# A hybrid retention and RG-LRU layer: branch outputs summed by accumulating transfers, first merge job in seven products, rotary exchanges on ScalarE

## The chip, the core and the metric

The kernel runs on one core of a Trainium2 chip. The metric is the time of one execution on the device in microseconds (us); all times here are in us unless marked ns. The engines are TensorE (PE; its weight loads are shown apart as PEld), VectorE (DVE), ScalarE (ACT), GpSimd (POOL) and SyncE (SP). SP, ACT and POOL also issue transfers (DMAs), each from a queue of its own, and 16 DMA engines carry them out.

## The reference, cut to what matters

One layer over 1024 positions (T) and 1024 channels (D), all in float32:

```python
h = rms_norm(x, norm1_w)
q, k, v, g_ret, x_lru, y_lru, gate_ret, gate_lru = split(h @ w_in)
q = rotary(q); k = rotary(k) * 128 ** -0.5        # 4 heads of 128; halves [x1*cos-x2*sin, x1*sin+x2*cos]
o = chunkwise_retention(q, k, v)                  # chunks of 64, decayed state
y_a = (head_group_norm(o) * silu(g_ret)) @ w_ret_o
hl = rg_lru(conv4(x_lru))                         # gates, scan over positions
y_b = (hl * gelu(y_lru)) @ w_lru_o
mix = sigmoid(gate_ret + b0) * y_a + sigmoid(gate_lru + b1) * y_b
x = x + mix @ w_out
up = rms_norm(x, norm2_w) @ ffn_w_up              # D_FF = 3072
gate, val = split(up)
x = x + (gelu(conv3(gate)) * val) @ ffn_w_down
return rms_norm(x, norm_f_w)
```

## The kernel before, in words

**Products.** Each dense projection is cut into jobs; a job has a left side of 256 rows (or channels) and an operand on the right, both in 2 by 2 blocks (A11 to A22, B11 to B22). A product of two blocks is twelve matmuls of 128x128 by 128x512 into a PSUM bank: four steps of the contraction, three passes each, since every float32 value is split into a high part (a cast on ACT, L458) and the rest (a subtraction on DVE, L459). `mm_by` (matmuls in L669) makes the eight plain products of a job. `mm_fast` (L703) makes seven: from the blocks it uses sums S1 to S4 of the left side (formed on DVE, L544 to L553) and T1 to T4 of the right side. Intermediate sums are copied out of PSUM on ACT (L742) and added on DVE (L721, L727, in `total`). Two jobs can go as a pair (`mate`), product by product in turn. The lists PRODS, FIRST and ENDING are orders of the seven products.

**Stages, in order.** A few warming matmuls on constants (L1459); norm statistics and the values v (L1429); q and k projections, the rotary step and the retention heads, beside the projections of the LRU branch, with its gates and scan; the retention output jobs (`ojobs` 0 to 3) and the LRU output jobs (`ojobs` 4 to 7); the merge jobs (`wjobs`, one for each t from 0 to 3) with w_out and the residual; the MLP's up and down jobs; the last norm.

**Around the change.** `rotary_head` swaps the two halves of 64 partitions of each q and k tile by two transfers from POOL (L1165, L1166), multiplies by cosine and sine and adds (L1167 to L1169); k is then transposed on PE (L1177). `emit_ret_o` multiplies a tile of the retention output by its gate and stores it in t1_d. `emit_lru_o` reads it back (L1356), multiplies the LRU output by its gate (L1375), adds the two (L1376) and stores the sum into mix_d (L1378), the left side of the merge jobs, which load it at L510. The first merge job (t = 0) is plain; the other three have seven products. The parameters of the first norm are loaded by ACT's queue (L1453); the first use is L1414. At the end, each pair of down tiles is weighted and squared (`square`: DVE L1850, ACT L1852 with a sum along the row, DVE L1859), the power -1/2 is taken on POOL (L1863), and the tiles are scaled and stored (L1868 to L1871).

**What sets the order.** The program is built twice. From the first build, the class `Plan` takes every instruction with its dependencies: `latest` works back from PE's order to the time at which each step is due, `forward` then schedules all engines by these due times (`rank`) with modelled durations, and its order is imposed on the second build. Each engine executes its list in order. Work in the smaller PSUM banks (tiles named a: retention, gates, transposes) stands ahead of the dense products on PE when both are ready. SBUF tiles come from the pools u (128x512 work tiles) and w (blocks); PSUM tiles g and a.

Of the kernel before, what the change touches and what calls it, by code (L numbers as in the profile page):

```python
# [18 lines left out]
P = 128  # L19
# [106 lines left out]
class Step:  # L126

    def __init__(self, ins):
# [71 lines left out]
class Plan:  # L200
# [6 lines left out]
    LATE_DMA, LATE_PE, BACKLOG, KEEP = 1500.0, 400.0, 300.0, 2000.0  # L207
    NEAR, APART = 500.0, 10000.0
# [97 lines left out]
    def forward(self, rank):  # L306
# [7 lines left out]
        moved, table = 0.0, None  # L314
# [9 lines left out]
        while left:  # L324
# [28 lines left out]
            order[e].append(n)  # L353
            left -= 1
# [20 lines left out]
        return order, max(free.values())  # L375

    def order(self, rounds=2):
        pe = [n for n, s in self.steps.items() if s.eng == "PE"]
        for _ in range(rounds):
# [35 lines left out]
def tile_trunk_layer(ctx, tc, x, xt, positions, params, consts, normf, w_in, w_v, w_ro, w_lo,  # L415
# [26 lines left out]
    t1_d = pdr.tile([KT, P, T], F32, tag="t1", name="t1_d")  # L442
# [28 lines left out]
    class Job:  # L471
        def __init__(self, src, op, emit, post=None, fast=False, last=False, drop12=False,
                     pre=None, fetch=None, order=None, ready=None, by=None, rate=RATE, mate=False,
                     prods=PRODS, stage=None):
            self.pre, self.ready, self.by, self.rate = pre, ready, by, rate
            self.stage = stage
# [210 lines left out]
    def mm_fast(group, op):  # L687
# [5 lines left out]
        banks, kept = {}, {}  # L693

        def prod(jb, bank, nm):
# [3 lines left out]
            n = 0  # L699
            for j in range(4):  # L700
                c = slice(128 * j, 128 * j + 128)
                for a, b in PASSES:
                    PE.matmul(bank, w[a][:, c], need(op, (SETS[nm], j))[b], start=first and n == 0, stop=n == 11,  # L703
                              skip_group_check=True)
                    n += 1
# [9 lines left out]
        def total(jb, nm, bank, m, c):  # L715
            if back3:
                nm = {"S3": "S2", "S2": "S3"}.get(nm, nm)
            u = kept.pop((jb, nm))
# [8 lines left out]
            V.tensor_add(u, bank, u)  # L727
            jb.emit(m, c, u, u)

        for i, nm in enumerate(plan):  # L730
            for jb in group:
# [6 lines left out]
                bank = banks[key]  # L738
                prod(jb, bank, nm)
# [613 lines left out]
    def from_sg_t1(n):  # L1353
        def fetch(m, h):
            t = get()
            SY.dma_start(t, t1_d[2 * n + m, :, TH * h:TH * h + TH])  # L1356
            return from_sg(1, n)(m, h), t
        return fetch

    def emit_ret_o(n):  # L1360
        def emit(m, h, ps, unit):
# [3 lines left out]
            ST.dma_start(t1_d[ch, :, TH * h:TH * h + TH], t)  # L1365
# [5 lines left out]
    def emit_lru_o(n):  # L1371
        def emit(m, h, ps, unit):
            ch = 2 * n + m
            g, t = ojobs[4 + n].take(m, h)
            V.tensor_mul(g, ps, g)  # L1375
            V.tensor_add(t, t, g)  # L1376
            put(g)
            ST.dma_start(mix_d[2 * h:2 * h + 2, :, ch // 4, :, ch % 4, :].rearrange("t m p c -> p (t m) c"),  # L1378
                         t.rearrange("p (q c) -> p q c", q=4))
            put(t)  # L1380
# [5 lines left out]
    def values():  # L1386
# [66 lines left out]
        nc.scalar.dma_start(par[:, 0:8], params[:, 0:8])  # L1453
# [164 lines left out]
    for n in range(4):  # L1618
        ojobs.append(Job(pair_src(w_lo, n), u, emit_lru_o(n), fast=True, last=n == 3, mate=n == 0,
                         fetch=from_sg_t1(n)))  # L1620
# [239 lines left out]

    def final(t, m, c):
# [18 lines left out]
    def down_post(g, t):  # L1880
        def fn():
# [3 lines left out]
            if g == 1 and t == 3:  # L1885
# [5 lines left out]
                 prods=ENDING if (g, t) == (2, 3) else PRODS,  # L1891
                 pre=((0, 0), (0, 1), (1, 1)), fetch=from_x1(t),
# [70 lines left out]
```

## Time and profile before

| What | Value |
|---|---|
| Median of 3 runs (lowest to highest) | 1580.0 (1579.94 to 1580.3) |
| The profiled execution's own time | 1582.15 |
| Span of its trace | 1580.4 |
| Mean granted TensorE clock | 0.998 |
| DMA packets | 160976, 286.30 MB |
| Swaps of half tiles from POOL's queue (u<-u, 32 of the 40 in the rotary step), 128 KB each: issue to landing | 3.5 |
| Writes of mix_d, 16 of 256 KB | 5.2 |

The profile's page gives for each engine its busy time, share and instructions. In the chain of work that ended last a row is: start, length, engine, tile and line, count. In a timeline a row is: start, busy time, engine (a q behind it: its issue of transfers), line, operation, tile written <- tiles read, size, count, and in brackets the engine's idle time before it with what ended that. A group's row has the count, then busy time and mean ns of one, then idle time before. A row of transfers ends with the KB of each and the us from issue to landing.

### The profile page before, as it was taken

How to read it: one execution, taken by the hardware profiler on the slowest of the kernel's cores; microseconds unless marked ns; L12 is line 12 of the kernel's file. 1: busy time of each engine (PE TensorE's matmuls, PEld its weight loads, DVE VectorE, ACT ScalarE, POOL GpSimd, SP SyncE). 2: the span in 40 equal slices, each digit the busy share in tenths (PEclk: the TensorE clock that was granted, in tenths of full speed). 3: DMA queues.
4: the chain of work that ended last, by engine and by line, in shares of the span. 5: the costliest groups of instructions: out<-in, count | busy, mean ns of one | idle time of the engine just before them, and what ended most of it. 6: DMA issues, size and time to landing. Idle time of an engine off the chain costs nothing.

```text
span 1580.4 us, 21535 instructions
## 1 busy us (share of the span) xinstructions
PE 1566.9 (99%) x7001; PEld 1293.2 (82%) x7001; DVE 1368.3 (87%) x2462; ACT 912.6 (58%) x1554; POOL 67.9 (4%) x105
## 2 busy tenths in 40 slices
PE   9999999999999999999999999999999999999998
PEld 7888888888888888888888888888888888888886
DVE  8999988897889998999997899777777778987885
ACT  7548845544459697955365765444444446563653
POOL 0001010011000000000000001000000000000000
PEclk9999999999999999999999999999999999999999
DMA  9344354464454345684996246444444456787752
GB/s 324 116 121 144 117 171 132 156 205 148 126 180 158 96 146 185 222 274 165 304 388 225 91 131 210 134 146 139 135 140 140 142 190 213 267 274 270 261 182 80
DMA packets 160976, 286.30 MB, mean 181 GB/s; under 512 B 17880, under 2 KB 30304, under 8 KB 160864
## 3 DMA queue, kind: packets, MB, share of 16 engines
q1 hardware_dynamic: 153664, 264.74, 51.3%
q0 software_dynamic: 5760, 17.83, 3.9%
q10 hardware_dynamic: 1440, 2.36, 0.5%
q8 instruction: 55, 0.90, 0.2%
q14 instruction: 57, 0.47, 0.1%
HBM read 195.73 MB, written 83.89 MB: 177 GB/s over the span
## 4 chain that ended last, share of the span: by engine, by line
PE 94%; ACT 2%; DMA 2%; DVE 1%; issue 1%; POOL 0%; SPq 0%; POOLq 0%; ACTq 0%; DVEq 0%
PE g L703 82%; PE g L1429 5%; PE a L1105 3%; PE g L669 1%; PE a L1214 1%; DMA u<-u 1%; PE a L1216 1%; PE a L1225 1%; PE a L1208 0%; PE a L1275 0%; DMA u<-td_d 0%; PE a L1695 0%; DMA w<-mix_d 0%; DMA u<-xt 0%; ACT u L458 0%
## 5 line engine op out<-in xcount | busy, mean ns | idle before, releaser
L703 PE MATMUL g<-u,w 128*128 128x512 f32 x5964 | 1390.3, 391 | 1.5 <-ACT u L742 1.1
L703 PEld LDWEIGHTS g<-u,w 128*128 128x128 f32 x5964 | 1114.2, 188 | 232.1 <-ACT u L742 3.1
L458 ACT CAST w<-w 128x512 fp32r<-128x512 f32 x516 | 317.2, 621 | 364.0 <-PE g L703 250.4
L459 DVE TENSOR_TENSOR w<-w,w 128x512 fp32r<-128x512 f32 x516 | 350.8, 686 | 62.1 <-ACT w L458 56.4
L727 DVE TENSOR_TENSOR u<-g,u 128x512 f32<-128x512 f32 x213 | 145.8, 687 | 46.9 <-PE g L703 40.4
L458 ACT CAST u<-u 128x512 fp32r<-128x512 f32 x233 | 138.6, 621 | 69.4 <-PE g L703 7.4
L742 ACT COPY u<-g 128x512 f32<-128x512 f32 x215 | 125.0, 582 | 64.5 <-PE g L703 62.0
L459 DVE TENSOR_TENSOR u<-u,u 128x512 fp32r<-128x512 f32 x233 | 153.1, 685 | 4.5 <-ACT u L458 4.4
L1744 DVE SCALAR_TENSOR_TENSOR u<-u,par,u 128x511 f32<-128x511 f32 (+1 forms) x96 | 71.5, 747 | 3.0 <-ACT u L1741 2.6
L1429 PE MATMUL g<-w,u 128*128 128x512 f32 x264 | 61.9, 390 | 0.9 <-DVE u L1414 0.7
L1429 PEld LDWEIGHTS g<-w,u 128*128 128x128 f32 x264 | 49.3, 188 | 12.1 <-ACT w L458 1.2
L1749 POOL DMA_DIRECT2D ff_d<-u x48 | 36.2, 754 | 451.2 <-DVE u L1748 442.5
L544 DVE TENSOR_TENSOR w<-w,w 128x512 f32<-128x512 f32 x71 | 48.7, 685 | 2.9 <-DMA w<-ff_d 1.7
L1105 PE MATMUL a<-u,u 128*128 128x512 f32 x192 | 50.9, 391 | 0.3 <-ACT u L458 0.3
L547 DVE TENSOR_TENSOR w<-w,w 128x512 f32<-128x512 f32 x71 | 48.7, 687 | 0.8
L553 DVE TENSOR_TENSOR w<-w,w 128x512 f32<-128x512 f32 x71 | 48.6, 685 | 0.2
L550 DVE TENSOR_TENSOR w<-w,w 128x512 f32<-128x512 f32 x71 | 48.6, 685 | 0.2
L1741 ACT ACTIVATE u<-u,par 128x512 f32<-128x512 f32 x48 | 39.3, 818 | 15.1 <-DVE u L727 15.0
L721 DVE TENSOR_TENSOR u<-u,u 128x512 f32<-128x512 f32 x45 | 30.8, 687 | 16.8 <-ACT u L742 15.8
L1105 PEld LDWEIGHTS a<-u,u 128*128 128x128 f32 x192 | 35.5, 188 | 8.9 <-ACT u L458 1.0
L1748 DVE TENSOR_TENSOR u<-u,u 128x512 f32<-128x512 f32 x48 | 33.0, 689 | 5.9 <-ACT u L1747 5.8
L1087 DVE SCALAR_TENSOR_TENSOR u<-u,par,u 128x511 f32<-128x511 f32 (+2 forms) x48 | 35.8, 746 | 0.0
(202 smaller groups left out, 1125.1 us busy)
## 6 DMA issues: line engine op xcount, KB each, us to landing
w<-w_in SPq DMA_DIRECT2D x96, 256.0 KB, 2.8
w<-w_up SPq DMA_DIRECT2D x96, 256.0 KB, 2.7
u<-w_dn SPq DMA_DIRECT2D x84, 256.0 KB, 3.8
u<-x_d SPq DMA_DIRECT2D x60, 256.0 KB, 4.3
x_d<-u SPq DMA_DIRECT2D x48, 256.0 KB, 3.6
ff_d<-u POOLq DMA_DIRECT2D x48, 256.0 KB, 2.7
td_d<-u SPq DMA_DIRECT2D x48, 256.0 KB, 3.0
u<-td_d SPq DMA_DIRECT2D x48, 256.0 KB, 4.9
```

Source lines behind the costliest of these rows:

```text
L458: S.copy(hi, src)
L459: V.tensor_sub(lo, src, hi.bitcast(F32))
L544: V.tensor_add(s, r["A21"], r["A22"])
L547: V.tensor_sub(s, s, r["A11"])
L550: V.tensor_sub(s, r["A12"], s)
L553: V.tensor_sub(src, r["A21"], r["A11"])
L703: PE.matmul(bank, w[a][:, c], need(op, (SETS[nm], j))[b], start=first and n == 0, stop=n == 11, skip_group_check=True)
L727: V.tensor_add(u, bank, u)
L742: S.copy(u, bank)
L1105: PE.matmul(ps, wg[g][a][:, cs], xs[k][b], start=q == 0, stop=q == 5)
L1429: PE.matmul(bank, o[p][:, c], w[q], start=first and j == n == 0, stop=j == 3 and n == 2, skip_group_check=True)
L1744: V.scalar_tensor_tensor(c[:, s:], src[:, :TH - s], w, c[:, s:], ALU.mult, ALU.add)
```

## The change

- The first merge job gets seven products in place of eight, as a pair with the second, in the order FIRST; w_out's blocks are loaded in the order B11, T3, B21, T1, T2, T4, B22 (sums that an earlier stage kept in tw_d are read from there).
- `emit_ret_o` stores into mix_d, from SP; `emit_lru_o` adds its product to it by an accumulating transfer from POOL. The tensor t1_d, its 16 reads and the 16 adds on DVE are gone.
- The exchange of the rotary step is two copies on ACT.
- The parameters of the first norm are loaded by POOL's queue.
- The last product of the last down job is made in two halves of 256 columns in two fresh banks, and the last tile's norm (`final_half`) follows half by half, with its squares on DVE.
- The planner: float32r matmuls last (n + 32) / 2.4 ns instead of a fixed 226.6; a transfer's reader may stand closer to it; due times are mapped onto the start times that `forward` found.

```diff
-                t = 226.6
+                t = (n + 32) / 2.4
...
+    SURE_DMA = 700.0
...
                 lag = self.lag(s, self.steps[m])
                 if lag is not None:
+                    if s.dma:
+                        lag = max(self.HAND + self.SURE_DMA, min(lag, rank[m] - done))
                     at[m] = max(at[m], done + lag)
...
-            span = -min(start[n] for n in pe)
-            rank = {n: t + span - (1e7 if self.steps[n].small else 0.0) for n, t in start.items()}
-            order, _ = self.forward(rank)
+            due = np.maximum.accumulate([start[n] for n in pe])
+            if begin is None:
+                begin = due - due[0]
+            names = list(start)
+            found = np.interp([start[n] for n in names], due, begin)
+            found += np.minimum([start[n] for n in names] - due[0], 0.0)
+            rank = {n: t - (1e7 if self.steps[n].small else 0.0) for n, t in zip(names, found)}
+            order, begin = self.forward(rank)
...
+            for s in jb.halves if nm == plan[-1] and jb.halves else (slice(0, TH),):
+                if nm == plan[-1] and jb.halves:
+                    bank, first = psg.get(), True
+                    parts.append((s, bank))
...
+            if parts:
+                for s, part in parts:
+                    V.tensor_add(jb.sum[:, s], part[:, s], jb.sum[:, s])
+                    final_half(jb.sum, s)
+                return
...
-                G.dma_start(w[0:64, :], t[64:128, :])
-                G.dma_start(w[64:128, :], t[0:64, :])
+                S.copy(w[0:64, :], t[64:128, :])
+                S.copy(w[64:128, :], t[0:64, :])
...
+    def into_mix(ch, h, t, q, **how):
+        q.dma_start(mix_d[2 * h:2 * h + 2, :, ch // 4, :, ch % 4, :].rearrange("t m p c -> p (t m) c"),
+                    t.rearrange("p (q c) -> p q c", q=4), **how)
...
             V.tensor_mul(t, ps, t)
-            ST.dma_start(t1_d[ch, :, TH * h:TH * h + TH], t)
+            into_mix(ch, h, t, ST)
...
-            g, t = ojobs[4 + n].take(m, h)
+            g = ojobs[4 + n].take(m, h)
             V.tensor_mul(g, ps, g)
-            V.tensor_add(t, t, g)
+            into_mix(ch, h, g, G, accum_op=ALU.add)
...
-        nc.scalar.dma_start(par[:, 0:8], params[:, 0:8])
+        G.dma_start(par[:, 0:8], params[:, 0:8])
...
-        builders.append(operand(wop, w_out_set, False))
-        builders.append(kept_sums(wop, tw_d))
+        builders.append(operand(wop, kept_or(w_out_set, tw_d), False, ("B11", "T3", "B21", "T1", "T2", "T4", "B22")))
...
-                 emit_out(t, t > 0), out_post(t), fast=t > 0, last=t == 3, drop12=t == 0,
-                 pre=((0, 0), (0, 1), (1, 1)), fetch=from_x(t), by=None if t else "k",
-                 order=None if t else ("A11", "A21", "A12", "A22"),
+                 emit_out(t, True), out_post(t), fast=True, last=t == 3,
+                 pre=((0, 0), (0, 1), (1, 1)), fetch=from_x(t), mate=t == 0, prods=FIRST if t < 2 else PRODS,
...
+        V.scalar_tensor_tensor(j[:, s], u[:, s], 1.0 / D, u[:, s], ALU.mult, ALU.mult, accum_out=two)
+        V.tensor_add(one, one, two)
+        V.tensor_mul(o[:, s], u[:, s], nf[1][:, s])
+        if s.start == 0:
+            return
+        G.tensor_tensor(r, one, half[:, 0:1], ALU.pow)
...
+                 halves=(slice(0, TH // 2), slice(TH // 2, TH)) if (g, t) == (2, 3) else (),
```

**The exchange.** Before, POOL's queue, where the first rotary tiles (u) of one head are swapped; each row names the tile written and the tile read, and in brackets what it waits for (DMAHW and DMASW are transfers, the others engines):

```order
L1166 DMA u_421_2356<-u_413_2151 64x512 [waits DMAHW2_49,DMAHW1_49,DMAHW3_49,DMASW0_49,DMAHW4_49,DVE_49,Activation_49]
L1165 DMA u_421_2356<-u_413_2151 64x512 [waits DMASW1_49]
L1166 DMA u_428_2430<-u_418_2271 64x512 [waits DMAHW2_49,DMASW2_49,DMAHW5_49,DVE_49,PE_49]
L1165 DMA u_428_2430<-u_418_2271 64x512 [waits DMASW3_49]
L1166 DMA u_426_2404<-u_420_2316 64x512 [waits DMASW6_49,DMASW7_49,DMASW5_49,DMAHW1_49,DMASW4_49,Activation_49]
L1165 DMA u_426_2404<-u_420_2316 64x512
```

After, ACT's list at such a place. L1189 and L1190 are the two copies, L766 is the copy out of PSUM (L742 before), L468 the cast of a block (L458 before):

```order
L825 ACTIVATE rs<-rs 128x4 [waits DVE_49]
L468 CAST w_567_3213<-w_550_3027 128x512 [waits DMAHW3_49,PE_49,Activation_49]
L766 COPY u_508_3198<-g_97_2963 128x512 [waits PE_49]
L468 CAST w_563_3167<-w_558_3110 128x512 [waits DVE_49]
L1190 COPY u_541_3401<-u_495_3008 64x512 [waits DVE_49]
L1189 COPY u_541_3401<-u_495_3008 64x512
L766 COPY u_519_3277<-g_97_2963 128x512 [waits DMAHW7_49,PE_49]
L468 CAST w_571_3252<-w_513_2822 128x512 [waits DVE_49]
```

The two halves now stand in ACT's list between casts and PSUM copies, and wait for DVE alone.

**The merge.** Before, SP's list where the last sums are stored into mix_d and loaded (tw_d: kept sums of w_out; sg_d: gates):

```order
L1378 DMA mix_d<-u_1446_7853 128x4x128 [waits DMAHW7_49,DVE_49]
L1314 DMA u_1524_8007<-tw_d 128x512 [waits DMAHW0_49]
L1638 DMA u_1530_8014<-x 128x512 [waits DMAHW1_49]
L1349 DMA u_1406_7792<-sg_d 128x512 [waits DMAHW2_49]
L1378 DMA mix_d<-u_1380_7709 128x4x128 [waits DMAHW3_49,DVE_49]
L1314 DMA u_1535_8051<-tw_d 128x512 [waits DMAHW4_49,PE_49]
L1314 DMA u_1539_8057<-tw_d 128x512 [waits DMAHW5_49,PE_49]
L1314 DMA u_1543_8063<-tw_d 128x512 [waits DMAHW6_49]
L510 DMA w_1365_7930<-mix_d 128x512 [waits DMAHW7_49]
L510 DMA w_1377_7950<-mix_d 128x512 [waits DMAHW0_49]
L510 DMA w_1369_7936<-mix_d 128x512 [waits DMAHW1_49]
L510 DMA w_1381_7958<-mix_d 128x512 [waits DMAHW2_49]
```

After, SP's list where the last blocks of mix_d are loaded (L1656 loads tiles of x):

```order
L1656 DMA u_1542_8081<-x 128x512 [waits DMAHW3_49,DVE_49]
L1656 DMA u_1528_8043<-x 128x512 [waits DMAHW4_49,PE_49]
L1656 DMA u_1548_8156<-x 128x512 [waits DMAHW5_49,DVE_49]
L1656 DMA u_1549_8180<-x 128x512 [waits DMAHW6_49,DVE_49]
L1656 DMA u_1559_8275<-x 128x512 [waits DMAHW7_49]
L520 DMA w_1373_7906<-mix_d 128x512 [waits DMASW5_49,DMAHW0_49,DMASW4_49,DMASW1_49]
L520 DMA w_1375_7910<-mix_d 128x512 [waits DMAHW1_49]
L520 DMA w_1374_7908<-mix_d 128x512 [waits DMAHW2_49]
L520 DMA w_1380_7928<-mix_d 128x512 [waits DMAHW3_49]
L1656 DMA u_1550_8201<-x 128x512 [waits DMAHW4_49,DVE_49]
```

and POOL's last accumulating transfers ahead of that:

```order
L1378 DMA mix_d<-u_1379_7753 128x4x128 [waits DMAHW6_49,DMASW4_49,DVE_49]
L1378 DMA mix_d<-u_1419_7827 128x4x128 [waits DMAHW2_49,DMASW5_49,DVE_49]
L1378 DMA mix_d<-u_1359_7678 128x4x128 [waits DMAHW7_49,DMASW6_49,DVE_49]
L1378 DMA mix_d<-u_1444_7866 128x4x128 [waits DMAHW0_49,DMASW7_49,DVE_49]
L1378 DMA mix_d<-u_1380_7755 128x4x128 [waits DMAHW3_49,DMASW0_49,DVE_49]
```

The stores have left SP, and the first of the four loads waits for three transfers of POOL's queue (DMASW).

**The end.** Before, the last rows of DVE's list (u and nst are the tiles of the last norm; the g tiles are PSUM):

```order
L1834 TENSOR_TENSOR u60_2956_15280<-g4_465_15155,u60_2956_15280 128x512 [waits DMAHW4_49,DMAHW0_49,PE_49]
L1850 TENSOR_TENSOR u12_2977_15317<-u60_2956_15280,u26_2833_14660 128x512 [waits DVE_49]
L1859 TENSOR_TENSOR nst_80<-nst_80 128x1 [waits Activation_49]
L727 TENSOR_TENSOR u80_2933_15240<-g1_468_15244,u80_2933_15240 128x512 [waits PE_49]
L1850 TENSOR_TENSOR u36_2990_15341<-u80_2933_15240,u57_2834_14662 128x512 [waits DVE_49]
L1859 TENSOR_TENSOR nst_80<-nst_80 128x1 [waits Activation_49]
L1868 TENSOR_SCALAR u36_2990_15341<-u36_2990_15341,nst_80 128x512 [waits Pool_49]
```

After, the same place. L734 adds a half of the last product, L1883 squares and sums, L1885 weights, L1884 adds the sums:

```order
L1850 TENSOR_TENSOR u71_2906_15226<-g5_463_15101,u71_2906_15226 128x512 [waits DMAHW7_49,DMAHW3_49,PE_49]
L1866 TENSOR_TENSOR u21_2927_15263<-u71_2906_15226,u22_2783_14606 128x512 [waits DVE_49]
L1875 TENSOR_TENSOR nst_79<-nst_79 128x1 [waits Activation_49]
L734 TENSOR_TENSOR u31_2883_15186<-g2_470_15275,u31_2883_15186 128x256 [waits PE_49]
L1883 SCALAR_TENSOR_TENSOR u6_2941_15303,nst_79<-u31_2883_15186 128x256 [waits DVE_49]
L1885 TENSOR_TENSOR u25_2940_15302<-u31_2883_15186,u75_2784_14608 128x256
L1884 TENSOR_TENSOR nst_79<-nst_79 128x1 [waits DVE_49]
L734 TENSOR_TENSOR u31_2883_15186<-g4_471_15288,u31_2883_15186 128x256 [waits PE_49]
L1883 SCALAR_TENSOR_TENSOR u6_2941_15303,nst_79<-u31_2883_15186 128x256 [waits DVE_49]
L1885 TENSOR_TENSOR u25_2940_15302<-u31_2883_15186,u75_2784_14608 128x256
L1884 TENSOR_TENSOR nst_79<-nst_79 128x1 [waits DVE_49]
L1893 TENSOR_SCALAR u25_2940_15302<-u25_2940_15302,nst_79 128x512 [waits Pool_49]
```

The last tile's one add, one weighting and one sum have become two of each, with the squares among them.

More of the change, by code (lines that the diff above doesn't have):

```diff
@@ L313, in forward @@
         order = {e: [] for e in self.ENGINES}
-        moved, table = 0.0, None
+        moved, table, begin = 0.0, None, []
         for n, k in todo.items():
@@ L353, in forward @@
             order[e].append(n)
+            if e == "PE":
+                begin.append(t)
             left -= 1
@@ L441, in tile_trunk_layer @@
     sg_d = pdr.tile([2, KT, P, T], F32, tag="sg", name="sg_d")
-    t1_d = pdr.tile([KT, P, T], F32, tag="t1", name="t1_d")
     x1_d = pdr.tile([T, D], F32, tag="x1", name="x1_d")
@@ L473, in __init__ @@
                      pre=None, fetch=None, order=None, ready=None, by=None, rate=RATE, mate=False,
-                     prods=PRODS, stage=None):
+                     prods=PRODS, stage=None, halves=()):
             self.pre, self.ready, self.by, self.rate = pre, ready, by, rate
-            self.stage = stage
+            self.stage, self.halves = stage, halves
             self.mate, self.prods = mate, prods
@@ L698, in prod @@
             first = nm in ("A11", "S4" if over else "S1", "A12")
[L699 to L705, printed above, removed]
+            for s in jb.halves if nm == plan[-1] and jb.halves else (slice(0, TH),):
+                if nm == plan[-1] and jb.halves:
+                    bank, first = psg.get(), True
+                    parts.append((s, bank))
+                n = 0
+                for j in range(4):
+                    c = slice(128 * j, 128 * j + 128)
+                    for a, b in PASSES:
+                        PE.matmul(bank[:, s], w[a][:, c], need(op, (SETS[nm], j))[b][:, s],
+                                  start=first and n == 0, stop=n == 11, skip_group_check=True)
+                        n += 1
             W.put(*w, late=SOONER)
@@ L727, in total @@
             V.tensor_add(u, bank, u)
+            if jb.halves and (m, c) == (0, 1):
+                jb.sum = u
+                return
             jb.emit(m, c, u, u)
@@ L738, in mm_fast @@
                 bank = banks[key]
+                if jb.halves and nm == "S4":
+                    total(jb, "S2", bank, 0, 1)
                 prod(jb, bank, nm)
@@ L1859, in square, with final_half @@
             V.tensor_add(nst[:, 2, 2 + m:3 + m], nst[:, 0, 2 + m:3 + m], nst[:, 1, 2 + m:3 + m])
+    def final_half(u, s):
+        one, two, r = nst[:, 0, 2:3], nst[:, 4, 0:1], nst[:, 3, 2:3]
+        if s.start == 0:
+            fin["o"], fin["j"] = get(), get()
+        o, j = fin["o"], fin["j"]
+        V.scalar_tensor_tensor(j[:, s], u[:, s], 1.0 / D, u[:, s], ALU.mult, ALU.mult, accum_out=two)
+        V.tensor_add(one, one, two)
+        V.tensor_mul(o[:, s], u[:, s], nf[1][:, s])
+        if s.start == 0:
+            return
+        G.tensor_tensor(r, one, half[:, 0:1], ALU.pow)
+        put(u, j)
+        for c in range(2):
+            t = fin.pop((0, 0)) if c == 0 else o
+            if c:
+                V.tensor_scalar(t, t, r, None, ALU.mult)
+            else:
+                S.activation(t, t, AF.Copy, scale=r)
+            (SY if c else nc.scalar).dma_start(out[128 * 3:128 * 4, TH * c:TH * c + TH], t)
+            put(t)
     def final(t, m, c):
```

16 lines of the change are left out of this document (4 added, 12 removed).

## The prediction

> **What bounds the kernel now.** I read first the head of the page, then the chain of work that ended last, then the timelines at the places that the diff touches. All times are microseconds.
>
> ```profile
> span 1580.4 us, 21535 instructions
> PE 1566.9 (99%) x7001; PEld 1293.2 (82%) x7001; DVE 1368.3 (87%) x2462; ACT 912.6 (58%) x1554; POOL 67.9 (4%) x105
> PE 94%; ACT 2%; DMA 2%; DVE 1%; issue 1%; POOL 0%; SPq 0%; POOLq 0%; ACTq 0%; DVEq 0%
> ```
>
> TensorE is busy for 1566.9 of 1580.4, and 94% of the chain runs through it. So two things alone can shorten this kernel: fewer or cheaper matmuls, or the 13.5 in which TensorE stands. The next row, of the chain, prices a matmul; the others, of the timeline, show where TensorE stands at the start and the end.
>
> ```profile
> 904.47 433.54 PE g L703 x1912
> 1.25 4.55 PE L1459 MATMUL a<-heat 128*128 128x512 bf16 x12 [1.25 <-DVE heat L1623]
> 6.55 5.71 PE L1429 MATMUL g<-w,u 128*128 128x512 f32 x22 [0.74 <-DVE u L1414]
> 1553.82 18.98 PE L703 MATMUL g<-u,w 128*128 128x512 f32 x83
> ```
>
> 433.54 / 1912 = 0.2267 for one matmul of 512 columns. TensorE waits 1.25 before the warming matmuls and 0.74 behind them, and it ends at 1553.82 + 18.98 = 1572.80, so 7.60 of the span lies behind it. Three waits in between, quoted below, make 0.95, 1.07 and 0.87. Together that is 12.48 of 13.5: what is left for the new planner to win anywhere else is about 1.0.
>
> **Part 1, the first merge job as seven products.** One product of twelve matmuls goes. TensorE is the bound on both sides of it: 12 x 0.2267 = **-2.72**. The four loads of w_out that go with it had no wait of their own.
>
> **Part 2, the norm weights from GpSimd's queue.**
>
> ```profile
> 0.74 0.41 ACTq L1405 DMA_DIRECT2D u<-xt  x1
> 1.18 0.45 ACTq L1453 DMA_DIRECT2D par<-params  x1
> 1.66 1.28 ACT L1456 ACT_TABLE_LOAD   x1 [1.66 <-PEq L1948]
> 5.92 0.48 DVE L1414 TENSOR_SCALAR u<-u,par 128x512 fp32r<-128x512 f32 x1 [4.72 <-DMA par<-params]
> par<-params ACTq DMA_DIRECT2D x1, 4.0 KB, 4.6
> u<-u POOLq DMA_DIRECT2D x40, 128.0 KB, 3.5
> ```
>
> The first real matmul waits for L1414, and L1414 for the parameters, issued at 1.18 as ScalarE's second transfer and landed 4.6 later. No small transfer from GpSimd stands in this trace. By its nearest row, the exchanges (3.5), and an issue at about 0.75, as ScalarE's first (0.74), the parameters land at 4.25. Then the warming matmuls, which end at 1.25 + 4.55 = 5.80, decide: the 0.74 is gone, **-0.74**. Ends: the longest landing of an exchange is 7.0 (quoted below), which from 0.75 ends at 7.75 instead of 5.8, +1.9; nothing earlier than 5.80 helps.
>
> **Part 3, the rotary exchanges on ScalarE.**
>
> ```profile
> 339.43 0.63 PE L1177 MATMUL a<-cst,u 128*128 128x128 f32 x4 [0.95 <-DVE u L1169]
> 402.54 0.66 PE L1177 MATMUL a<-cst,u 128*128 128x128 f32 x4 [1.07 <-DVE u L1169]
> L458 ACT CAST u<-u 128x512 fp32r<-128x512 f32 x233 | 138.6, 621 | 69.4 <-PE g L703 7.4
> 230.00:440.00 210.00, 207.99 (x995) 173.96 (x994) 181.59 (x414) 98.21 (x186) 13.36 (x26) 1.00 0.50 154
> DMA to landing us min/median/max: 2.5/4.2/7.0
> ```
>
> (The fourth row is the table of windows: length, then busy time of PE, PEld, DVE, ACT and POOL, clock, DMA share, GB/s; the last is the landing of the exchanges of L1165.) Twice TensorE stands before a transpose of a rotated tile, because an exchange lands late. A pair of copies takes about 2 x 0.62 = 1.24, by ScalarE's SBUF-to-SBUF cast of as many columns (half the partitions, which I count for nothing), where the transfer took 4.2 in the middle. Both waits should close: 0.95 + 1.07 = **-2.02**. The price is 32 x 0.62 = 19.8 of ScalarE's time, in a window where it is busy for 98.2 of 210; with them it is 118 of 210, so TensorE's work covers it. The cover is gone where a copy waits in ScalarE's order with a copy out of PSUM behind it: ends 0 and, if every one of the eight tiles costs TensorE a copy's 0.62, +5.0. DVE keeps its three instructions for each tile.
>
> **Part 4, the chain into the merge.** Now DVE no longer adds the two branches: the LRU product goes into mix_d by an accumulating transfer, and the merge loads wait for it.
>
> ```profile
> 793.76 0.61 PE L669 MATMUL g<-u,w 128*128 128x512 f32 x2
> 794.62 0.58 ACT L742 COPY u<-g 128x512 f32<-128x512 f32 x1
> 795.25 5.76 PE L703 MATMUL g<-u,w 128*128 128x512 f32 x24 [0.87 <-ACT u L742]
> 799.06 0.68 DVE L1375 TENSOR_TENSOR u<-g,u 128x512 f32<-128x512 f32 x1
> 800.26 0.69 DVE L1376 TENSOR_TENSOR u<-u,u 128x512 f32<-128x512 f32 x1
> 800.97 0.37 SPq L1378 DMA_DIRECT2D mix_d<-u  x1
> mix_d<-u SPq DMA_DIRECT2D x16, 256.0 KB, 5.2
> w<-mix_d SPq DMA_DIRECT2D x16, 256.0 KB, 5.3
> ff_d<-u POOLq DMA_DIRECT2D x48, 256.0 KB, 2.7
> ```
>
> The old order's wait of 0.87 in front of the merge goes with that order. What is late next is the second half of mix for rows 0 to 255. From the end of the matmuls of LRU channel block 7 (first rows) the chain is: PE to its reader 0.25 (794.37 to 794.62), multiply 0.68, issue 0.02 (800.95 to 800.97), the accumulating transfer, the load 5.3, a sum of two blocks on DVE 0.69, its cast 0.62, and three hand-overs at an estimated 0.1 each: 7.86 plus the transfer. In the new PE order 55 matmuls stand between those and the first product that reads it: 55 x 0.2267 = 12.47 of cover. No accumulating transfer is in the trace. With the old write of the same tile, 5.2, the chain is 13.06 and TensorE waits 0.6; net of 0.87 **-0.27**. Ends: a landing like ff_d's of the same shape on the same queue, 2.7, leaves no wait (-0.87); twice the old write, 10.4, gives 7.86 + 10.4 - 12.47 = 5.8, net +4.9. I take 5.2, since the same stage's load decides it. Queued behind an accumulate on GpSimd are only more accumulates; behind the four waiting loads on SP, loads of x for the sums of the merge, which are late by as much.
>
> **Part 5, the last product in halves.**
>
> ```profile
> 1571.66 0.16 DVE L1859 TENSOR_TENSOR nst<-nst 128x1 f32<-128x1 f32 x1
> 1572.84 0.69 DVE L727 TENSOR_TENSOR u<-g,u 128x512 f32<-128x512 f32 x1 [1.02 <-PE g L703]
> 1575.04 0.16 DVE L1859 TENSOR_TENSOR nst<-nst 128x1 f32<-128x1 f32 x1 [0.79 <-ACT a L1852]
> 1575.28 0.54 POOL L1863 TENSOR_TENSOR nst<-nst,half 128x1 f32<-128x1 f32 x1 [2.78 <-DVE nst L1859]
> 1575.86 0.72 ACT L1870 ACTIVATE u<-u,nst 128x512 f32<-128x512 f32 x1 [0.85 <-POOL nst L1863]
> 1576.61 0.34 ACTq L1871 DMA_DIRECT2D out<-u  x1
> L1229 DVE SCALAR_TENSOR_TENSOR state<-state,a 128x256 f32<-128x256 f32 x24 | 9.8, 410 | 0.5 <-PE a L1225 0.4
> L926 DVE DVE_READ_ACCUMULATOR a<-u 128x1 f32 x8 | 1.1, 141 | 0.0
> L703 PEld LDWEIGHTS g<-u,w 128*128 128x128 f32 x5964 | 1114.2, 188 | 232.1 <-ACT u L742 3.1
> ```
>
> With the first half ready half a product early, DVE starts at 1571.82, when the last norm step of the tile before it ends, and works through two halves: 2 x (add 0.41 + square 0.41 + read-out 0.14 + weight 0.41 + sum 0.16) = 3.06, and nine gaps of 0.03: 1575.15, against 1575.20 now. The sum, the power and the scaling behind it stay: **-0.05**. That holds if 24 matmuls of 256 columns cost half each, 24 x 0.113 = 2.72. If the weight load sets the pace, 24 x 0.188 = 4.51; the second half then ends at 1574.59 instead of 1572.80, and DVE's second half at 1576.29: +1.1. A gain of more than 0.3 is excluded by DVE's own row of work.
>
> **Part 6, the planner.** The new table moves retention work a few dozen matmuls earlier and lets a reader stand closer to its transfer (0.7 instead of up to 1.5). I count it as nothing: at most 1.0 is to be won, and five readers that each come 0.8 early would lose 4. Two more activation table loads (1.28 each, by the row quoted in part 2) lie in ScalarE's idle time.
>
> **Sum:** -2.72 - 0.74 - 2.02 - 0.27 - 0.05 = -5.80. The span becomes 1574.6. The profiled execution took 1582.15 with its 1580.4 of span, the median of the runs is 1580.0; a change in the span carries over: **1574.2**.
>
> **Rivals.**
>
> **(a) The accumulating transfers fill the transfer engines: slower.**
>
> ```profile
> q1 hardware_dynamic: 153664, 264.74, 51.3%
> q0 software_dynamic: 5760, 17.83, 3.9%
> 690.00:780.00 90.00, 90.00 (x399) 74.52 (x398) 89.05 (x148) 43.87 (x76) 0.00 (x0) 1.00 0.74 244
> 780.00:840.00 60.00, 59.13 (x260) 48.39 (x259) 52.66 (x88) 35.10 (x66) 0.72 (x1) 1.00 1.05 380
> ```
>
> 256 KB take all 16 engines 0.513 x 1580.4 x 0.262 / 264.74 = 0.80 on SP's queue and 0.91 on GpSimd's. From 780 to 840 the share is 1.05: here there is no room. The change takes out 16 reads, 16 writes and 4 loads, 36 x 0.80 = 28.8, and puts in 16 accumulates of an unknown length e. At e up to 1.8, twice a plain one, it breaks even. Slower by over 0.2% (3.2, about what a measurement of this kernel can tell from no change) needs the whole gain of 5.8 eaten and 3.2 more, 9.0 of transfer time: e = (28.8 + 9.0) / 16 = 2.4, three times a plain one. At four times, 3.2, the excess is 16 x 3.2 - 28.8 = 22 and the time 1596, less what the emptier stage before 780 takes up. For it: pieces of 512 bytes, each read and written. Against it: the loads fall by 20, and the share before 780 is 0.74. Chance 0.11.
>
> **(b) ScalarE's order takes back what the exchanges gave.** The copies stand in one queue with the casts and the PSUM copies; the two waits return as waits for ScalarE, and the planner's closer readers add one or two. Then the gain of part 3 is nil and 1 to 4 are lost: 1577 to 1580, said as 1578. For it: ScalarE is in order. Against it: its idle 112 of 210. Chance 0.20.
>
> **(c) Descriptors written late.** DVE is busy 89.05 of 90 before the merge. If GpSimd's transfers are held while DVE works, an accumulate lands like the slowest exchange, 7.0: the chain is 14.86, the wait 2.4 instead of 0.6, the time 1576.0. For it, 7.0 with DVE at 86%; against it, ff_d's 2.7 with as busy a DVE. Chance 0.08. The Trainium skill states such a rule on its page "SBUF — State Buffer", section "Who interferes with whom": GpSimd must write the descriptors of its transfers, and DVE in a two-port mode locks it out, which two-tensor operations do not do. By that rule part 4 would cost 1.8 more than by the row of 5.2; ff_d's row speaks against it, and no run here isolates it.
>
> **(d) The halves are bound by weight loads**: +1.1, 1575.3, inside the forecast's own spread.
>
> **How the numbers follow.** The forecast with its spread, 1572.5 to 1576.5, has 0.53; better than that, by a shorter merge chain and the planner's 1.0, 0.08; (c) 0.08; (b) 0.20; (a) 0.11. Faster by over 0.2% means below 1576.8: 0.53 + 0.08 + 0.08 = 0.69. Within it: 0.20. Slower: 0.11. The range, 1571.5 to 1581.5, leaves out (a)'s slow end, the merge chain's 10.4 together with another loss, and a sliver below.
>
> **What would show it.** 24 fewer matmuls of 512 columns and 24 of 256 in their place; the first matmul behind the warming ones at about 5.8 instead of 6.55; no idle time before the transposes of rotated tiles; the wait before the first merge product that reads the second half of mix (0.6), and the landing of the accumulates beside 5.2; the transfer share around the merge; the last product's matmuls at 0.113 each and the last output's issue near 1571. I am wrong if the accumulates take more than 2.4 of engine time, if ScalarE becomes the releaser in front of TensorE, or if TensorE's idle time grows at places that the diff does not name.

## The result, and the profile after

The changed kernel takes 1592.89 (median of 4 runs, 1591.83 to 1594.84), the kernel before 1580.15 (1579.94 to 1581.64): a ratio of 1.0078, 95% interval 1.0066 to 1.0091. It is slower by 12.7, where 5.8 less had been forecast, and outside the range of 1571.5 to 1581.5. The profiled execution took 1591.83 with a span of 1590.1, 9.7 more than before.

The head of the page and the queue of GpSimd's transfers:

```profile
span 1590.1 us, 21467 instructions
PE 1569.2 (99%) x7001; PEld 1295.0 (81%) x7001; DVE 1368.9 (86%) x2464; ACT 934.1 (59%) x1588; POOL 72.9 (5%) x90
q0 software_dynamic: 12704, 17.83, 5.0%
```

The slices of the page show where to look: the granted TensorE clock is 9 in every slice but one, around 800. TensorE's timeline there (start, busy time, operation, count, and in brackets the idle time ahead with its releaser):

```profile
763.68 24.53 PE L717 MATMUL g<-u,w 128*128 128x512 f32 x107
796.38 21.91 PE L717 MATMUL g<-u,w 128*128 128x512 f32 x84 [8.17 <-ACT u L766]
822.03 8.24 PE L717 MATMUL g<-u,w 128*128 128x512 f32 x28 [3.73 <-ACT w L468]
```

Two waits, 8.17 and 3.73, stand where the kernel before has one of 0.87. And the matmuls behind them are slow: 84 in 21.91 are 2.87 more than 84 x 0.2267, and 28 in 8.24 are 1.89 more. The windows of the trace (length, then busy time of PE, PEld, DVE, ACT and POOL, clock, DMA share, GB/s) put it on the granted clock, which is 0.50 in the 5 us behind the first wait and 0.57 in the mean of the 4 behind the second:

```profile
796.40:801.40 5.00, 5.00 (x12) 3.93 (x13) 5.00 (x10) 3.57 (x7) 0.98 (x1) 0.50 1.05 387
801.70:817.90 16.20, 16.20 (x72) 13.41 (x71) 11.43 (x20) 8.90 (x16) 5.11 (x4) 0.99 1.14 255
822.00:826.00 4.00, 3.97 (x10) 3.04 (x11) 3.99 (x7) 3.56 (x7) 0.00 (x0) 0.57 1.02 379
```

Who makes TensorE wait? ScalarE's timeline and its waits in this stage (what it waited for: us in total, times, longest):

```profile
777.10 0.57 ACT L766 COPY u<-g 128x512 f32<-128x512 f32 x1
789.32 0.62 ACT L468 CAST w<-w 128x512 fp32r<-128x512 f32 x1 [11.64 <-DMA w<-mix_d]
...
795.75 0.57 ACT L766 COPY u<-g 128x512 f32<-128x512 f32 x1
```

ScalarE stands for 11.64 at the cast of a block of mix. The copy out of PSUM that TensorE's next product needs (795.75) is behind it in the list, with nine more casts between. That block is late because its load is issued at 782.34 and lands 6.9 later; the load stands in SP's list behind loads that wait for accumulates in flight (first row, SP's waits; run 10 shows that the data would have held it as long), and the accumulates land late (second and third row: the transfers of the whole trace and the landings of the lines of L1378, stores from SP included):

```profile
SPq L1355 <- DMA mix_d<-u: 7.4, 1, 7.4
mix_d<-u POOLq DMA_DIRECT2D x16, 256.0 KB, 8.4
DMA to landing us min/median/max: 2.3/6.0/13.1
```

The second wait is the chain that the prediction had worked out, here from the chain of work that ended last:

```profile
807.14 8.42 DMA mix_d<-u
...
815.70 4.91 DMA w<-mix_d
820.61 0.02 issue
820.63 0.70 DVE w L554
821.34 0.02 issue
821.36 0.63 ACT w L468
821.98 0.04 issue
822.03 8.01 PE g L717 x27
```

Accumulate 8.42, load 4.91, sum 0.70, cast 0.63, and TensorE goes on. The other parts of the change, at the start, in the retention stage and at the end:

```profile
1.25 5.30 PE L1477 MATMUL a<-heat 128*128 128x512 bf16 x12 [1.25 <-DVE heat L1641]
1.28 0.71 POOL L1471 DMA_DIRECT2D par<-params  x1 [0.83 <-POOLq L1987]
5.89 0.49 DVE L1432 TENSOR_SCALAR u<-u,par 128x512 fp32r<-128x512 f32 x1 [4.69 <-DMA par<-params]
230.00:440.00 210.00, 210.00 (x1007) 176.14 (x1007) 184.21 (x420) 118.46 (x218) 0.00 (x0) 1.00 0.45 144
1580.51 0.69 DVE L1850 TENSOR_TENSOR u<-g,u 128x512 f32<-128x512 f32 x1 [0.59 <-PE g L717]
1581.74 1.60 PE L717 MATMUL g<-u,w 128*128 128x256 f32 x12
1582.12 0.42 DVE L734 TENSOR_TENSOR u<-g,u 128x256 f32<-128x256 f32 x1
```

The parameters land at 5.89, as before. The warming matmuls end at 1.25 + 5.30 = 6.55, where the prediction had 5.80. In the retention stage TensorE is busy for 210.00 of 210 (207.99 before). From the add of the last whole product (1580.51; 1570.12 in the trace before) to the end of the span it is 1590.1 - 1580.51 = 9.59, and 1580.4 - 1570.12 = 10.28 before. The 24 half matmuls lie in this stretch: they start at about 1580.45 and end at 1581.74 + 1.60 = 1583.34, 0.12 each.

| Part | Forecast | From the two traces |
|---|---|---|
| 12 matmuls fewer | -2.72 | -2.72 |
| Start | -0.74 | -0.03 (6.52 for 6.55) |
| Exchange: the two waits | -2.02 | -2.02 |
| Merge: waits (8.17 + 3.73 for 0.87) | -0.27 | +11.03 |
| Merge: half clock behind them (2.87 + 1.89) | not foreseen | +4.76 |
| End, the 24 halves included | -0.05 | -0.69 |
| Sum | -5.80 | +10.33; the span shows +9.7, and the 0.6 between them was not placed |

### The profile page after: what moved, and what is told of

Read it like the earlier page. It is cut to its first block, busy times and chain, and to the rows that moved or that the text cites. A ratio compares the mean times of both kernels' runs of the same rounds, so it can differ in the third digit from the quotient of the medians.

```text
span 1590.1 us, 21467 instructions
## 1 busy us (share of the span) xinstructions
PE 1569.2 (99%) x7001; PEld 1295.0 (81%) x7001; DVE 1368.9 (86%) x2464; ACT 934.1 (59%) x1588; POOL 72.9 (5%) x90
## 3 DMA queue, kind: packets, MB, share of 16 engines
q0 software_dynamic: 12704, 17.83, 5.0%
## 4 chain that ended last, share of the span: by engine, by line
PE 47%; issue 2%; DMA 1%; DVE 1%; POOL 1%; ACT 0%; POOLq 0%; SPq 0%; ACTq 0%; DVEq 0%
PE g L717 47%; POOL mix_d L1378 1%; DMA mix_d<-u 1%; DMA u<-sg_d 1%; PE a L1713 0%; DVE w L469 0%; DMA w<-mix_d 0%; DVE u L1396 0%; DVE u L469 0%; DVE u L1385 0%; ACT u L468 0%; DVE u L746 0%; ACT u L1722 0%; DVE w L554 0%; DVE u L920 0%
## 5 line engine op out<-in xcount | busy, mean ns | idle before, releaser
L717 PE MATMUL g<-u,w 128*128 128x512 f32 x6060 | 1413.2, 392 | 12.5 <-ACT u L766 8.4
L717 PEld LDWEIGHTS g<-u,w 128*128 128x128 f32 x6060 | 1133.9, 188 | 246.6 <-ACT u L766 9.9
L468 ACT CAST w<-w 128x512 fp32r<-128x512 f32 x519 | 318.3, 621 | 368.1 <-PE g L717 250.1
L766 ACT COPY u<-g 128x512 f32<-128x512 f32 x218 | 126.9, 582 | 66.7 <-PE g L717 64.9
L468 ACT CAST u<-u 128x512 fp32r<-128x512 f32 x229 | 134.7, 620 | 52.5 <-PE g L717 5.3
L1378 POOL DMA_DIRECT2D mix_d<-u x16 | 20.5, 1400 | 657.6 <-DVE u L1396 638.0
```

Of the source, the lines that this page charges most:

```text
L468: S.copy(hi, src)
L717: PE.matmul(bank[:, s], w[a][:, c], need(op, (SETS[nm], j))[b][:, s], start=first and n == 0, stop=n == 11, skip_group_check=True)
L766: S.copy(u, bank)
```

## The experiments

The theories at the outset. **A:** an accumulating transfer is slow, and what waits for it makes both waits. **B:** the pair of seven-product jobs asks for mix too early, however it is written. **C:** the new planner puts readers too close to their transfers. Each run's kernel is the changed one, but for the edit shown. The runs of the kernel before beside them had medians of 1580.80 (the first four), 1581.24 (the next four) and 1581.33 (the last four); ratios are to those runs, with 95% intervals.

**1. Plain writes in place of the accumulates.** The retention branch is missing from mix. Every engine's list is the same, row by row and buffer by buffer, as in the changed kernel; the 16 transfers alone differ.

```diff
-            into_mix(ch, h, g, G, accum_op=ALU.add)
+            into_mix(ch, h, g, G)
```

> The changed kernel with the 16 accumulating transfers as plain writes from the same queue, at the same place of every engine's list; it leaves the retention branch out of mix. Theory A (an accumulating transfer is slow: about 2.0 us of all 16 transfer engines instead of 0.9, landing 8.8 in the merge instead of about 5): the two waits of TensorE in the merge (8.2 and 3.7) shrink to under 2 together, the granted clock there stays at 1.00, and the time falls to 1574 to 1578. Theory B (the pair of seven-product jobs asks for mix too early, and ScalarE stands before the cast of a block of mix with TensorE's copies behind it, however the transfer writes): both waits stay over 8 together and the time stays at 1588 or above.

Measured: 1578.88, ratio 0.9986 (0.9977 to 0.9995). GpSimd's queue, the landing of its writes, and TensorE in the merge:

```profile
q0 software_dynamic: 5536, 17.83, 3.6%
mix_d<-u POOLq DMA_DIRECT2D x16, 256.0 KB, 5.3
789.30 4.38 PE L717 MATMUL g<-u,w 128*128 128x512 f32 x18 [1.44 <-ACT u L766]
794.21 15.26 PE L717 MATMUL g<-u,w 128*128 128x512 f32 x66 [0.52 <-ACT u L766]
810.43 19.86 PE L717 MATMUL g<-u,w 128*128 128x512 f32 x85 [0.97 <-ACT w L468]
```

The waits are 1.44, 0.52 and 0.97, the 85 matmuls behind the last one run at 0.234. One word in one line is worth 14.0: theory A holds, since neither order nor buffers differ. The time is still not 1574; 2.9 of waits remain that the kernel before does not have in this form.

**2. The add on DVE again** (t1_d, its reads, the stores from SP).

```diff
-            into_mix(ch, h, g, G, accum_op=ALU.add)
+            V.tensor_add(t, t, g)
+            into_mix(ch, h, t, ST)
```

> The changed kernel with the two branches added on DVE as before (t1_d, its 16 reads and the plain stores from SP are back), all else as changed, planner included. Theory A: 1573 to 1577, since the seven products, the exchange and the halves keep what they gave (2.7 + 2.0 + 0.7) and only the accumulates go. Theory B: 1585 or above, since the pair still asks early.

Measured: 1580.54, ratio 0.9996 (0.9986 to 1.0005): between the two forecasts. The accumulates cost 12 by this run too (1592.89 beside 1580.54), but the 5.4 of gains is not seen. One wait and a slow stretch behind it (2.17 more than 146 x 0.2267) show where most of it goes, in TensorE's timeline of this run:

```profile
795.04 35.27 PE L718 MATMUL g<-u,w 128*128 128x512 f32 x146 [2.12 <-ACT u L767]
```

**3. Eight products again, accumulates kept** (`mm_by` for the first merge job, w_out loaded as before).

```diff
-                 emit_out(t, True), out_post(t), fast=True, last=t == 3,
+                 emit_out(t, t > 0), out_post(t), fast=t > 0, last=t == 3, drop12=t == 0,
```

> The changed kernel with the first merge job plain again (eight products, w_out and its kept sums loaded as before), the accumulates kept. Theory A: the loads of mix still wait for late accumulates, so TensorE still stands for 8 or more in the merge: 1590 to 1597. Theory B: the waits go, and the time is 1577 to 1581.

Measured: 1593.13, ratio 1.0079 (1.0062 to 1.0096). TensorE's timeline of this run has the waits with plain products (L679) too:

```profile
795.36 4.55 PE L717 MATMUL g<-u,w 128*128 128x512 f32 x12 [6.85 <-ACT u L766]
821.13 9.12 PE L679 MATMUL g<-u,w 128*128 128x512 f32 x29 [4.20 <-ACT w L468]
```

Theory B is not what made the loss.

**4. The planner of before.**

```diff
-                t = (n + 32) / 2.4
+                t = 226.6
...
-                        lag = max(self.HAND + self.SURE_DMA, min(lag, rank[m] - done))
```

(and the due times as before). 

> The changed kernel with the planner of before (226.6 ns a matmul, readers 1.5 us behind a transfer, due times not mapped onto the schedule). Theory A: the accumulates are as slow, 1588 to 1596. Theory C (the new planner puts readers too close to their transfers, the cast of mix ahead of TensorE's copies on ScalarE above all): the waits go and the time is 1575 to 1580.

Measured: 1590.14, ratio 1.0057 (1.0042 to 1.0072), with waits of 8.31 and 3.84. Theory C falls; the new planner is worth at most some 3 of the loss.

**5 and 6. The add on DVE with the old planner, and with eight products.** The edits of run 2 with those of run 4, and of run 2 with those of run 3.

> The branches added on DVE as before, and the planner of before; seven products, exchange on ScalarE, parameters from GpSimd and halves stay. With the add on DVE and the new planner the span was 1579.3, with 1.7 more idle time of TensorE before 232 than the kernel before, and 4.0 lost at 787 to 800. If the new planner's order makes both: 1574 to 1576. If the pair of seven-product jobs makes the wait at 790 whatever the planner: 1577 to 1579.

> The branches added on DVE as before and the first merge job plain again; the new planner, the exchange, the parameters and the halves stay. If the pair of seven-product jobs makes the wait of 2.3 and the slower clock behind it: no wait at 790, and the time is that of the same kernel with the pair, plus 2.7, less up to 4: 1578 to 1580 beside 1580. If the wait has another cause (the planner, the sums of mix): 1582 to 1584.

Measured: 1581.96, ratio 1.0009 (0.9999 to 1.0018), though the profiled execution was the fastest of its ten runs (span 1577.4); and 1579.62, ratio 0.9991 (0.9982 to 1.0001). Neither forecast of the first fits its median. (The forecast puts 1.7 more idle time of TensorE before 232 in run 2; the waits there are 1.25, 0.74 and 0.50, beside 1.25 and 0.74 in the kernel before, so it is 0.5.) TensorE's timeline of the first, where waits stay in the merge:

```profile
793.07 14.80 PE L711 MATMUL g<-u,w 128*128 128x512 f32 x64 [1.43 <-ACT u L760]
810.88 19.49 PE L711 MATMUL g<-u,w 128*128 128x512 f32 x84 [3.00 <-ACT w L462]
```

and of the second (L680 is the plain job), where they nearly go:

```profile
793.20 5.75 PE L718 MATMUL g<-u,w 128*128 128x512 f32 x24 [0.62 <-ACT u L767]
798.78 9.23 PE L680 MATMUL g<-u,w 128*128 128x512 f32 x40
```

So the pair's waits don't come from the planner. The kernel with twelve matmuls more is no slower than run 2 (1579.62 beside 1580.54): the pair gives its saving of 2.72 back in its waits and the slow matmuls behind them. That its shorter cover makes these waits fits the counts given below, but no run shows it by itself.

**7. The planner told the price of an accumulate.** Theory **D**: the 8.17 comes from the place of the cast in ScalarE's list, which the planner chose because it takes an accumulate for a plain write.

```diff
-                    done = t + s.hold + self.landing(s)
+                    done = t + s.hold + self.landing(s) + (6000.0 if add else 0.0)
```

> The changed kernel with a planner that counts an accumulating transfer as 6 us later landed and 2.5 times the transfer time. Theory D (the cost is the place of the cast of mix in ScalarE's list, ahead of TensorE's copies, because the planner takes an accumulate for a plain write): the wait of 8.2 falls below 2 and the time to 1578 to 1583. Theory A alone (the full transfer engines hold the loads wherever the readers stand): 1588 or more.

Measured: 1585.10, ratio 1.0024 (1.0014 to 1.0033). TensorE's timeline:

```profile
791.87 16.62 PE L720 MATMUL g<-u,w 128*128 128x512 f32 x72 [0.91 <-ACT u L769]
811.56 1.31 PE L720 MATMUL g<-u,w 128*128 128x512 f32 x4 [3.07 <-ACT w L471]
814.17 16.11 PE L720 MATMUL g<-u,w 128*128 128x512 f32 x59 [1.31 <-DVE w L472]
```

ScalarE's list now has the first cast of mix behind the copy for the product after the wait:

```profile
791.24 0.58 ACT L769 COPY u<-g 128x512 f32<-128x512 f32 x1
791.72 0.62 ACT L471 CAST w<-w 128x512 fp32r<-128x512 f32 x1
```

The 8.17 is 0.91 although the accumulates land as late (9.0): D is right for the first wait. All lists were laid out anew, so other rows have moved with the cast. The time is 2 above its forecast, because the second wait stays, 3.07 and 1.31, with 59 matmuls in 16.11 behind it (2.7 too long).

**8. Rows of 2 KB.**

```diff
-    mix_d = pdr.tile([4, 2, 2, P, 4, P], F32, tag="mix", name="mix_d")
+    mix_d = pdr.tile([KT, 2, P, TH], F32, tag="mix", name="mix_d")
```

> The changed kernel with mix_d laid out by channel block, so that an accumulating transfer adds rows of 2 KB and the merge's loads gather pieces of 512 bytes. If an accumulate pays for each piece (12704 packets on its queue beside 5536 with plain writes): landing near 5, GpSimd's issue near 0.75 instead of 1.3, both waits together under 4, the time 1577 to 1583. If it pays for its bytes: landing and waits stay and the time is 1588 or more.

Measured: 1590.79, ratio 1.0059 (1.0044 to 1.0074). GpSimd's queue and its landing by the page and the list of transfers, and TensorE's first wait by its timeline:

```profile
q0 software_dynamic: 6560, 17.83, 4.4%
mix_d<-u POOLq DMA_DIRECT2D x16, 256.0 KB, 7.2
795.42 22.01 PE L718 MATMUL g<-u,w 128*128 128x512 f32 x84 [6.78 <-ACT u L767]
```

The packets halve and the transfer time per accumulate falls (below), but it still lands at 7.2 in the middle and the waits are 6.78 and 2.73. Less transfer time alone does not remove the waits. How much it would be worth is not shown, since the loads of mix, now in pieces of 512 bytes, land at 6.4 in the middle instead of 4.9.

**9. Work in the wait.** The product ahead of the 8.17 is computed four times over: 36 matmuls, 8.2 us.

```diff
+                for again in range(4 if jb is ojobs[7] and nm == "A12" else 1):
```

> The changed kernel with one product (A12 of the last LRU output job, the last that TensorE runs before its wait of 8.2) computed four times over, each time anew into the same bank: 36 matmuls, 8.2 us, of useless work. If the slower clock after a wait is caused by the wait (matmuls at 0.43 instead of 0.227 for about 5 us after 8.6 of idling), the useless work lies in the wait, the clock behind it stays at full speed, and the span falls by 2 to 3 from 1590.1. If the clock falls for another reason, the span stays, and if the wait is not one for a transfer but grows with TensorE's work, it rises by up to 8.

Measured: 1597.22, ratio 1.0096 (1.0079 to 1.0112), span 1595.6: neither 2 less nor 8 more. TensorE's timeline, and the window behind its first wait with the clock (1.00):

```profile
797.58 4.60 PE L718 MATMUL g<-u,w 128*128 128x512 f32 x19 [0.42 <-ACT u L767]
805.68 16.66 PE L718 MATMUL g<-u,w 128*128 128x512 f32 x65 [3.50 <-ACT u L767]
826.47 3.83 PE L718 MATMUL g<-u,w 128*128 128x512 f32 x10 [4.12 <-ACT w L468]
797.60:801.60 4.00, 4.00 (x18) 3.31 (x19) 3.07 (x6) 1.42 (x3) 0.57 (x1) 1.00 1.04 362
```

The useless work fills the wait, and the clock behind it is 1.00 instead of 0.50: the half clock is made by the wait. But a new wait of 3.50 opens 19 matmuls later, again behind ScalarE, with its own slow stretch. Why that one opens was not followed up; the order of the lists differs from the changed kernel's.

**10. Sources of the accumulates kept apart.** Theory **E**: the wait in SP's list for a buffer makes the first wait.

```diff
-            put(g)
+            put(g, late=30)
```

> The changed kernel with the tiles that feed the accumulates handed back to their pool later, so that the loads of the kept sums of w_out take other buffers and don't stand in SP's list behind an accumulate's landing (7.4 there). Theory E (the 8.2 comes from SP's list: the first four loads of mix stand behind a load that waits for the buffer of an accumulate in flight): the four loads are issued at about 778 instead of 782 to 784.6, the wait falls by 3 or more, and the time to 1583 to 1588. If the data dependence alone makes it (the loads wait for the last accumulates of the first half anyway): same as the changed kernel, 1589 to 1593.

Measured: 1590.86, ratio 1.0063 (1.0048 to 1.0078). The waits of SP's queue and of ScalarE from 764 to 815:

```profile
SPq L520 <- DMA mix_d<-u: 8.9, 1, 8.9
ACT w L468 <- DMA w<-mix_d: 11.7, 1, 11.7
```

SP no longer waits for a buffer ahead of the loads; it waits 8.9 at the load itself. Theory E falls: the data make the load wait as long as the buffer did.

**11. Exchange and halves alone:** the edits of runs 2, 3 and 4 together, and the parameters on ScalarE's queue again.

> The kernel before with two parts of the change alone: the exchange on ScalarE and the last product in halves; the add on DVE, eight products, parameters and planner as before. By the traces the exchange is worth the two waits of 1.1 and 1.2 and the halves 0.7: span 1577.2 (1576.5 to 1578.5), that is 3 below the kernel before, faster than both kernels. If ScalarE's list takes the exchange's gain back elsewhere: within 1 of the kernel before.

Measured: 1578.29, ratio 0.9983 (0.9973 to 0.9992), span 1575.8: 0.17% faster than the kernel before, and faster than the changed one. Of TensorE's timeline, the one wait that is left in the merge:

```profile
792.44 5.73 PE L711 MATMUL g<-u,w 128*128 128x512 f32 x24 [0.38 <-ACT u L760]
```

**12. All three remedies:** the edits of runs 7, 8 and 10.

> The changed kernel with all that was found against the accumulates: rows of 2 KB, the planner's price for them, and their sources kept apart. If buffers, place in ScalarE's list and engine time were the whole cost: no wait over 2 in the merge, 1576 to 1580. If the second half's chain (accumulate 7 to 8, load 5) stays longer than its cover of 55 matmuls: a wait of 3 to 5 and a slower clock of 1 to 2.5 behind it remain: 1581 to 1585.

Measured: 1583.17, ratio 1.0012 (1.0002 to 1.0021), as the second forecast had it. The landing of the accumulates, and TensorE's second wait:

```profile
mix_d<-u POOLq DMA_DIRECT2D x16, 256.0 KB, 6.2
812.36 0.73 PE L721 MATMUL g<-u,w 128*128 128x512 f32 x2 [3.38 <-ACT w L471]
814.26 16.04 PE L721 MATMUL g<-u,w 128*128 128x512 f32 x58 [1.17 <-ACT w L471]
```

At the best found here the accumulate is 2.6 slower than the read and the add on DVE that it replaces (run 2): the chain of the second half stays longer than its cover.

## Why the prediction was wrong

**Part 4 failed**, the step "what is late next is the second half of mix". Its chain was right, and one term was mis-sized: the accumulate was set at 5.2, "since the same stage's load decides it", and took 8.42. With the measured 8.42 the prediction's own sum gives 7.86 + 8.42 - 12.47 = 3.81; TensorE waited 3.73, and 55 matmuls do stand in the trace between the two products (806.0 to 818.3). The end of 10.4 that was kept for the range covers this.

What was missing altogether is the **first half of mix**. The prediction asked who waits for the accumulates on GpSimd and on SP, but not who stands behind the first loads of mix on ScalarE: a cast, and behind it the PSUM copies that TensorE needs for the LRU jobs still running. Run 7 moves that cast, and 8.17 becomes 0.91 with accumulates as slow. So the larger wait takes two things: a transfer that lands late (run 1) and an in-order list that had been laid out for an early one (run 7). The row of 8.17 is also one of the prediction's own signs of being wrong: ScalarE as the releaser in front of TensorE.

The **half clock** was missing too: 4.76, which run 9 puts on the waits. The Trainium skill, "TensorE: Matmul & The Clock Gate", section "HAM oscillation — how this bites in real kernels", says that a gap in TensorE's work of more than about 3.4 us brings its clock down to half. The 0.50 behind 8.17 agrees. Shorter waits go both ways here: behind the 2.12 of run 2 the granted clock is 0.50 from 797 to 799, and behind the 3.00 in run 5's profile it stays at 1.00 (84 matmuls in 19.49, 0.232 each).

**Rival (a)** had the right sign by another mechanism. It priced the transfer engines' time: breaking even at 1.8 for each accumulate, slower from 2.4. GpSimd's queue took 5.0% x 1590.1 = 79.5 with accumulates and, in run 2 without them, 2.9% x 1579.3 = 45.8: 2.1 each, below its threshold, and 0.7 as plain writes in run 1 (56.8 - 45.8 over 16). By its own sum 2.1 costs 16 x 2.1 - 28.8 = 4.8 of the gain of 5.8, and the kernel would still be a little faster; the landing and what stands behind it in the lists make the rest. Run 8 brings the 2.1 to 1.5 (69.9 - 45.8 over 16) and gains 2. The full engines are not cleared, though: from 764 to 815 the four loads of mix landed at 8.0 in the middle, and the eight in run 1, with the same lists, at 5.1.

**Part 1** was right as a count of matmuls and wrong as a gain. The cover that the plain job gave (65 matmuls in the same place, by the old order) was worth about as much as the product, 55 matmuls of cover being left: run 6 against run 2.

**Part 3** was right: both waits closed, ScalarE's busy time rose to 118.46 (118 forecast), and rival (b) did not come about. **Part 2** was mis-sized: GpSimd issues at 1.28, not 0.75, and the parameters land 4.6 later, as from ScalarE's queue, not 3.5. The other bound, the end of the warming matmuls at 5.80, does not hold either: the twelve took 5.30 here, 4.55 before and 4.05 in run 5. **Part 5** gained 0.69 for 0.05: the halves cost 0.12 a matmul (not bound by the weight load, 0.188), and DVE's instructions overlap, so that two halves took from 1582.12 to 1584.67, 2.55 instead of 3.33. **Part 6**: whether the new planner helps or harms stays open; runs 2 and 5 differ by less than their runs scatter. **Rival (c)**, descriptors held up by DVE, is not told apart here; the plain writes of run 1 landed at 5.3 from the same queue beside the same DVE work, which speaks against it.

Not tried: a merge chain with more cover (an order of products that takes the second half of mix later), and accumulates issued for the first half alone.

## What to carry to other kernels

A transfer that replaces a read and an add is paid for in its landing time, so cost it as a link of every chain that waits for it, the early one too, and ask in each in-order list what stands behind the first reader. Where the order of work is computed from prices, a new kind of operation needs its price first. A removed product is worth its matmuls only if its time was not the cover of a transfer; and a wait of TensorE of 2 us or more may cost about 2 to 3 again in slow matmuls (2.87, 1.89, 2.17 and 2.7 here, 0.4 behind the 3.00 of run 5).

## What the runs showed of the hardware that was not expected

An accumulating transfer of 128 rows x 4 pieces of 512 bytes took GpSimd 1.28 to issue, where the plain write of the same shape took 0.75; it landed at 8.4 in the middle (up to 13.1) beside 5.3, took 2.1 of all 16 transfer engines beside 0.7, and put (12704 - 5536) / 16 = 448 more packets on its queue. Pieces of 2 KB brought this to 7.2, 1.5 and 6560 packets in all.

A 4 KB load issued from GpSimd's queue took as long to land (4.6 in the changed kernel, 4.0 to 5.0 over the runs) as from ScalarE's (4.6 before, 5.0 in run 11). And 36 matmuls put into a wait of TensorE kept its clock at 1.00 behind it.
